# The softmax bias as a minimum of negatively scaled scores, with the query's norm held in that scale in the sparse attention

## The chip, the core and the metric

The kernel runs on one core of a Trainium2 chip. The core has a matrix engine (TensorE, "PE" in the rows; "PEld" is its weight load), a vector engine (VectorE, "DVE"), an activation engine (ScalarE, "ACT"), a slower general engine (GpSimd, "POOL") and queues that move data between main memory and the on-chip memory (SBUF); matrix products land in a small accumulator memory (PSUM). Each engine runs its own list of instructions in the order in which the program issued them, and waits where an operand or a buffer isn't ready. The metric is the device time of one execution in microseconds (us).

## What is computed

Two decoder layers on 256 tokens of width 1024, with 16 heads of 64. Layer 0 is a feed-forward half step, a mixture of three causal dilated attentions, and a feed-forward half step. A shared set of keys and values follows, and layer 1 is a feed-forward half step, native sparse attention (NSA: compressed, selected and sliding-window branches, two groups of key heads) and a last feed-forward half step. The lines that the change touches are these:

```python
# dilated attention: one softmax for each block of 128 queries
s = jnp.einsum('nhqd,nhkd->nhqk', qb, kb).astype(jnp.float32) * scale      # scale = 64 ** -0.5
s = jnp.where(band & (start - front + ki >= 0), s, -jnp.inf)
m = jnp.max(s, axis=-1, keepdims=True)
p = jnp.exp(s - m)
den = jnp.sum(p, axis=-1, keepdims=True)

# sparse attention: queries are normed per head, and a rotated copy feeds two of three branches
q = rms_norm(qg[..., :hdim].reshape(b, s, N_HEADS, HEAD_DIM), q_gain)
q_nope = to_grp(q)                 # compressed branch
q_rope = to_grp(rope(q))           # selected and sliding-window branches
ss = jnp.einsum('bkgqd,bkqnd->bkgqn', qr, ks).astype(jnp.float32) * scale
p_s = masked_softmax(ss, (kpos <= t[:, None])[:, :, None])
sw = jnp.einsum('bkgqd,bknd->bkgqn', qr, kw).astype(jnp.float32) * scale
p_w = masked_softmax(sw, wband & (start - SLIDE_WINDOW + ki >= 0))
```

The norm of a head is one number for each query and head: q times that number, then rotated, is the same as q rotated, then multiplied by it.

## The kernel before

Tokens lie on the 128 partitions in two tiles (`tt` or `qt`, 0 and 1). A matrix product of two float32 operands is made of three products of high and low parts, so each weight tile of 128x1024 needs a cast to its high part (ACT, line 387) and a subtraction for its low part (mostly DVE, line 413). These, and the reductions that form the adaptive scales from `w_ada` (DVE, line 393), are the background work between which all other DVE and ACT work stands.

**Order.** The program is written by a planner, class `_Clock`. A task is a generator that yields (engine, estimated time, buffers taken and given); the planner always steps the task that can start first by its estimates, and `pick` chooses among engines by the earliest estimated end. The order in which instructions are issued is each engine's final order. So an edit that alters one estimate or leaves out one step can move others.

**Dilated attention** (about 240 to 560 us of the span): for eight pairs of heads and two query tiles `dil_unit` makes two score tiles of 128x512 in PSUM; DVE adds the mask and takes the row maximum in one custom instruction each (line 975, with a second instruction that reads the accumulator out); DVE multiplies the two maxima by -SCALE into `nb` (line 980); ACT takes exp(SCALE·y + nb) (line 983); then 1/sum (989), scaling (991), transposes on PE (906) copied back by ACT (912) or DVE (914), and the value product (1007). `qk_task` prepares queries and keys of a head group: squares (ACT 860), sums (DVE 864), a root by three Newton steps of four POOL instructions (581, 584, 585, 586), the rotated copies (DVE 890, 894, POOL 895) scaled by that root on POOL (938), transposes on PE (906).

**Sparse attention** (about 980 to 1090 us): `q_task` handles a group of eight heads. It takes the squares and sums, runs the same Newton steps on POOL to `rs`, scales the queries for the compressed branch on DVE (N, inside line 1329) and transposes them (1348). For each token tile a `q_rope` task rotates the unnormed queries on DVE (890, 894, 895), waits until `rs` is there, scales the rotated copy (R, also line 1329, on POOL or DVE as `pick` finds), casts the high part on ACT (1379), subtracts for the low part (1383, POOL or DVE by `pick`) and transposes both (1389); PSUM is copied out by line 1358 on ACT or line 1360 on DVE, again by `pick`. `cmp_scores` does the compressed branch (PE 1406, DVE 1410 to 1427), which also needs the product of line 1531 (DVE). `units(kv)` starts eight `nsa_unit` tasks for each key group when both rotated tiles are ready: four score tiles (PE 1448, n = 128 or 256 columns), the mask and row maximum (DVE 1455), `nb` for all four (DVE 1458), exp (ACT 1461), 1/sum times a gate (DVE 1465, 1468), scaling by that (POOL 1478 or DVE 1475), transposes (PE 1485), value products (PE 1504).

Of the kernel before, what the change touches and what calls it, by code (L numbers as in the profile page):

```python
# [14 lines left out]
AF = mybir.ActivationFunctionType  # L15
ALU = mybir.AluOpType
# [34 lines left out]
RL = 0  # L51
# [12 lines left out]
P = 128  # L64
# [159 lines left out]
class _Kernel:  # L224
# [732 lines left out]
    def dil_unit(self, hg, hp, qt, oh, ol):  # L957
# [4 lines left out]
        mx, den = self.small(2, "mx"), self.small(2, "den")  # L962
# [340 lines left out]
    def q_task(self, kv, ps):  # L1303
# [15 lines left out]
        st = {"rs": None, "at": 0.0, "reads": 0}  # L1319
# [8 lines left out]
        def scaled(eng, o, i, tt):  # L1328
            eng.tensor_tensor(out=o, in0=i, op=ALU.mult,
                              in1=st["rs"][:, tt * 8:(tt + 1) * 8].unsqueeze(2).to_broadcast([P, 8, HD]))  # L1330

        for tt in range(TT):
            clk.spawn(self.q_rope(kv, tt, ps[tt], qr, st, read, scaled), RL)
        yield "G", 3200.0
        st["rs"] = self.head_newton(x, y, 16)
        st["at"] = clk.free["G"] + clk.lag
        N = []
        for tt in range(TT):
            yield "V", 610.0
            N.append(self.tmp((P, 8, HD)))  # L1340
            scaled(nc.vector, N[tt], ps[tt].rearrange("p (h d) -> p h d", d=HD), tt)
# [20 lines left out]
    def q_rope(self, kv, tt, ps, qr, st, read, scaled):  # L1362
# [73 lines left out]
    def nsa_unit(self, kv, pr, qt, oh, ol):  # L1436
# [15 lines left out]
        mx, den = self.small(4, "mx4"), self.small(4, "den4")  # L1452
# [407 lines left out]
```

## Time and profile before

| | |
|---|---|
| time before, median of 3 runs | 1301.76 us (1300.01 to 1302.33) |
| the profiled execution's own time | 1301.44 us |
| its span in the trace | 1299.7 us |
| PE, DVE, ACT, POOL busy | 1219.7 (94%), 975.8 (75%), 646.0 (50%), 258.0 us (20%) |
| span by stage | feed-forward 0 to 240, dilated 240 to 560, feed-forward, shared keys and feed-forward 560 to 980, sparse 980 to 1080, rest to 1299.7 |

The span is the stretch from the first to the last recorded instruction; 1.74 us of the execution's own time lie around it. All times below count from the span's start. In rows of instructions the columns are the start, the duration, engine, line and operation, the tiles written and read, shapes, and in brackets the engine's idle time before it with what released it.

### The profile page before, as it was taken

To read this page: it belongs to the slowest core of one execution; us is meant where nothing else is said; L and a number is where in the kernel's file an instruction comes from. 1 tells how busy PE (TensorE), PEld (TensorE's weight loads), DVE (VectorE), ACT (ScalarE), POOL (GpSimd) and SP (SyncE) were. 2 spreads that over 40 slices of the span, in tenths; PEclk is the share of its full clock that TensorE was granted. 3 is DMA by queue.
4 is the path that set the end of the run, shared out by engine and by line. 5 is a ranking of instruction groups with operands and counts; after the bars stand their busy time and mean duration, and the time that the engine had idled before them with its cause. 6 is when DMAs were issued, how large, how long until landed. Compare 5 with 4: busy or idle time off the path is not lost.

```text
span 1299.7 us, 23375 instructions
## 1 busy us (share of the span) xinstructions
PE 1219.7 (94%) x9373; PEld 1140.8 (88%) x9373; DVE 975.8 (75%) x1743; ACT 646.0 (50%) x1126; POOL 258.0 (20%) x356
## 2 busy tenths in 40 slices
PE   4799999789989898899999999999999889999998
PEld 3799999667777687799999999989998778999998
DVE  6799886866758677578888878878878997766652
ACT  4545454435445354456455446545435477654431
POOL 3480010462433525210000100030001353000000
PEclk9999999999899899899999999999999899999999
DMA  8889886543454534245988956776883003466650
GB/s 323 285 328 353 314 317 259 201 163 154 143 191 151 196 130 162 97 163 181 340 321 324 341 213 244 279 279 248 343 305 135 33 2 132 163 257 232 242 192 17
DMA packets 42733, 284.50 MB, mean 219 GB/s; under 512 B 5249, under 2 KB 6273, under 8 KB 9346
## 3 DMA queue, kind: packets, MB, share of 16 engines
q1 hardware_dynamic: 42626, 283.02, 58.9%
q8 instruction: 73, 1.20, 0.4%
q14 instruction: 34, 0.28, 0.1%
HBM read 281.96 MB, written 1.05 MB: 218 GB/s over the span
## 4 chain that ended last, share of the span: by engine, by line
PE 73%; DVE 12%; POOL 9%; ACT 3%; issue 2%; DMA 1%; SPq 0%; ACTq 0%; DVEq 0%; POOLq 0%
PE mm L466 18%; PE mm L467 18%; PE mm L468 18%; PE mm L849 3%; PE mm L850 3%; PE mm L851 3%; DVE wl L413 2%; POOL y L938 2%; PE tp L906 2%; POOL rs_t L584 2%; POOL rs_t L581 2%; POOL rs_y L586 2%; POOL rs_t L585 1%; DVE y L1455 1%; DVE st L393 1%
## 5 line engine op out<-in xcount | busy, mean ns | idle before, releaser
L413 DVE TENSOR_TENSOR wl<-st,wh 128x1024 fp32r<-128x1024 f32 x361 | 436.1, 1234 | 93.4 <-ACT wh L387 93.0
L387 ACT CAST wh<-st 128x1024 fp32r<-128x1024 f32 x361 | 369.0, 1049 | 133.8 <-PE mm L468 46.6
L466 PE MATMUL mm<-uh,wh 128*128 128x256 f32 x1304 | 364.6, 280 | 1.4 <-DVE y L738 1.4
L467 PE MATMUL mm<-uh,wl 128*128 128x256 f32 x1304 | 364.5, 280 | 0.0
L468 PE MATMUL mm<-ul,wh 128*128 128x256 f32 x1304 | 363.4, 279 | 0.0
L466 PEld LDWEIGHTS mm<-uh,wh 128*128 128x128 f32 x1304 | 245.0, 188 | 1.7 <-DVE y L738 1.6
L467 PEld LDWEIGHTS mm<-uh,wl 128*128 128x128 f32 x1304 | 245.1, 188 | 0.1
L468 PEld LDWEIGHTS mm<-ul,wh 128*128 128x128 f32 x1304 | 245.2, 188 | 0.0
L466 PE MATMUL mm<-y,wh 128*128 128x256 f32 x832 | 233.5, 281 | 0.1
L467 PE MATMUL mm<-y,wl 128*128 128x256 f32 x832 | 232.4, 279 | 0.0
L468 PE MATMUL mm<-y,wh 128*128 128x256 f32 x832 | 231.8, 279 | 0.0
L393 DVE CUSTOM_DVE_ANT_0 st<-st,cact 128x1024 f32<-128x1024 f32 x152 | 187.0, 1259 | 0.0
L466 PEld LDWEIGHTS mm<-y,wh 128*128 128x128 f32 x832 | 156.4, 188 | 1.1 <-issue 0.9
L467 PEld LDWEIGHTS mm<-y,wl 128*128 128x128 f32 x832 | 156.4, 188 | 0.0
L468 PEld LDWEIGHTS mm<-y,wh 128*128 128x128 f32 x832 | 156.4, 188 | 0.0
L849 PE MATMUL mm<-wh,uh 128*128 128x512 f32 (+1 forms) x336 | 137.1, 408 | 0.0
L850 PE MATMUL mm<-wl,uh 128*128 128x512 f32 (+1 forms) x336 | 132.4, 394 | 0.0
L851 PE MATMUL mm<-wh,ul 128*128 128x512 f32 (+1 forms) x336 | 131.7, 392 | 0.0
L524 POOL TENSOR_TENSOR y<-y 128x256 f32<-128x256 f32 x20 | 22.7, 1137 | 351.9 <-ACT y L505 351.9
L895 POOL TENSOR_TENSOR y<-y 128x512 f32<-128x512 f32 (+1 forms) x26 | 32.3, 1251 | 267.3 <-DVE y L894 157.2
L849 PEld LDWEIGHTS mm<-wh,uh 128*128 128x128 f32 x336 | 67.2, 200 | 14.2 <-issue 1.3
L851 PEld LDWEIGHTS mm<-wh,ul 128*128 128x128 f32 x336 | 66.9, 199 | 13.8
(254 smaller groups left out, 1622.0 us busy)
## 6 DMA issues: line engine op xcount, KB each, us to landing
st<-w_in SPq DMA_DIRECT2D x88, 1024.0 KB, 5.1
st<-w_ada SPq DMA_DIRECT2D x76, 1024.0 KB, 5.5
st<-w_out SPq DMA_DIRECT2D x44, 1024.0 KB, 6.4
st<-w_qk SPq DMA_DIRECT2D x24, 1024.0 KB, 4.9
st<-w_va SPq DMA_DIRECT2D x8, 1024.0 KB, 4.8
st<-w_o SPq DMA_DIRECT2D x8, 1024.0 KB, 4.9
st<-w_vb SPq DMA_DIRECT2D x4, 1024.0 KB, 5.5
st<-w_q SPq DMA_DIRECT2D x4, 1024.0 KB, 6.4
```

The costliest lines, as they stand in the source:

```text
L387: nc.scalar.copy(out=wh, in_=src)
L393: nc.vector.tensor_tensor_reduce(out=src, in0=src, in1=self.cact, scale=1.0, scalar=0.0, op0=ALU.mult, op1=ALU.add, accum_out=self.mod[:, ...
L413: (self.nc.gpsimd if eng == "G" else self.nc.vector).tensor_tensor(out=o, in0=src[:, c], in1=i.bitcast(F32), op=ALU.subtract)
L466: mm(out=out, lhsT=ah, rhs=bh, start=start, stop=False, **kw)
L467: mm(out=out, lhsT=al, rhs=bh, start=False, stop=False, **kw)
L468: mm(out=out, lhsT=ah, rhs=bl, start=False, stop=stop, **kw)
L581: eng.tensor_tensor(out=t, in0=y, in1=y, op=ALU.mult)
L584: eng.tensor_tensor(out=t, in0=t, in1=x, op=ALU.mult)
L849: mm(out=ps[tt], lhsT=uh[k][:, c], rhs=wh[:, o], start=k == 0, stop=False)
L850: mm(out=ps[tt], lhsT=uh[k][:, c], rhs=wl[:, o], start=False, stop=False)
L851: mm(out=ps[tt], lhsT=ul[k][:, c], rhs=wh[:, o], start=False, stop=k == KC - 1)
L895: (eng or nc.gpsimd).tensor_tensor(out=A, in0=A, in1=B, op=ALU.add)
```

## The change

In the dilated attention the masked score is now formed with the immediate scale -SCALE and reduced by a minimum, which is `nb` itself; the multiplication of line 980 is gone and the exponent's scale is -1. In the sparse attention the same happens with the scale read from a column of a table, `qscale`, which holds -SCALE times the query's root. The rotated queries aren't scaled any more: the rope task doesn't wait for the root, and units wait until `qscale` is written. POOL writes `qscale` in one 128x16 instruction behind the Newton steps. The queries of the compressed branch are scaled on DVE as before.

```diff
@@ dil_unit
-            nc.vector.tensor_tensor_reduce(out=st, in0=scs[e], in1=self.dmask[:, qt], scale=1.0, scalar=-3e38,
-                                           op0=ALU.add, op1=ALU.max, accum_out=mx[:, e:e + 1])
+            nc.vector.tensor_tensor_reduce(out=st, in0=scs[e], in1=self.dmask[:, qt], scale=-SCALE, scalar=3e38,
+                                           op0=ALU.add, op1=ALU.min, accum_out=nb[:, e:e + 1])
             sts.append(st)
             T = clk.V(512, clk.now)
-        nb = self.small(2, "nb")
-        nc.vector.tensor_scalar(out=nb, in0=mx, scalar1=-SCALE, scalar2=None, op0=ALU.mult)
-        T = clk.on("V", 70, T)
         for e in range(2):
-            nc.scalar.activation(out=sts[e], in_=sts[e], func=AF.Exp, bias=nb[:, e:e + 1], scale=SCALE,
+            nc.scalar.activation(out=sts[e], in_=sts[e], func=AF.Exp, bias=nb[:, e:e + 1], scale=-1.0,
@@ q_task
         yield "G", 3200.0
-        st["rs"] = self.head_newton(x, y, 16)
-        st["at"] = clk.free["G"] + clk.lag
+        rs = self.head_newton(x, y, 16)
+        nc.gpsimd.tensor_scalar(out=self.qscale[kv], in0=rs, scalar1=-SCALE, scalar2=None, op0=ALU.mult)
+        self.scaled[kv] = True
@@ q_rope
-        while st["rs"] is None or clk.now < st["at"]:
-            yield st["at"] if st["rs"] else clk.now + 100.0
-        w = clk.pick(0, G=1010.0, V=610.0)
-        yield w
-        scaled(nc.vector if w[0] == "V" else nc.gpsimd, R, R, tt)
@@ nsa_unit
+        head = qt * 8 + pr * 2
         for e, b, c, i in blocks:
-            nc.vector.tensor_tensor_reduce(out=sts[e][:, c], in0=scs[e][:, c], in1=self.amask[:, S - n:S], scale=1.0,
-                                           scalar=-3e38, op0=ALU.add, op1=ALU.max, accum_out=mx[:, i:i + 1])
-        nb = self.small(4, "nb4")
-        nc.vector.tensor_scalar(out=nb, in0=mx, scalar1=-SCALE, scalar2=None, op0=ALU.mult)
+            nc.vector.tensor_tensor_reduce(out=sts[e][:, c], in0=scs[e][:, c], in1=self.amask[:, S - n:S],
+                                           scale=self.qscale[kv][:, head + e:head + e + 1],
+                                           scalar=3e38, op0=ALU.add, op1=ALU.min, accum_out=nb[:, i:i + 1])
@@ units
-            while self.ready[kv] < TT or not self.keys:
+            while self.ready[kv] < TT or not self.scaled[kv] or not self.keys:
```

Where instructions stand now, by engine. Line numbers shift: 1217 before is 1214 after, 1348 is 1343, 1389 is 1379, 1383 is 1373, 1406 is 1396, 1448 is 1438, 1478 is 1468, 1485 is 1475, 989 is 986, 991 is 988. Over the whole program DVE issues 1701 instructions instead of 1743, among them 32 fewer `nb` and three fewer PSUM copies of line 1360 (ACT takes these); one unit's four multiplications (1475) and one pair of subtractions (1383) go from DVE to POOL.

**PE in the sparse attention, behind the second projection of queries.** Before, eight transposes of one unit and four of the next, of 128 columns (1485, one row of twelve), stand ahead of the compressed scores (1406):

```order
L1217 MATMUL tp<-ident,y 128x128 x2
L849 MATMUL mm<-wh,uh 128x512
L850 MATMUL mm<-wl,uh 128x512
L851 MATMUL mm<-wh,ul 128x512
L1448 MATMUL sc<-shareA,y 128x512
L1448 MATMUL sc<-y 128x512
L1448 MATMUL mm<-shareA,y 128x512
L1448 MATMUL mm<-y 128x512
L1485 MATMUL tp<-ident,y 128x128 x12
L1406 MATMUL sc<-shareB,y 128x32 x8
L1348 MATMUL tp<-ident,y 128x128 x4
L1389 MATMUL tp<-ident,y 128x128 x4
```

and after:

```order
L1214 MATMUL tp<-ident,y 128x128 x2
L1438 MATMUL sc<-shareA,y 128x512
L1438 MATMUL sc<-y 128x512
L1438 MATMUL mm<-shareA,y 128x512
L1438 MATMUL mm<-y 128x512
L1475 MATMUL tp<-ident,y 128x128 x8
L1379 MATMUL tp<-ident,y 128x128 x4
L1396 MATMUL sc<-shareB,y 128x32 x8
L1343 MATMUL tp<-ident,y 128x128 x4
L1379 MATMUL tp<-ident,y 128x128 x4
L1438 MATMUL sc<-shareA,y 128x256
```

The first four transposes of the rotated queries (1389, after 1379) have moved ahead of the compressed scores and ahead of the normed queries' transposes (1348); the next unit's four transposes have left this place.

**POOL at the same place**, the end of the Newton steps (rs_t, rs_y) and what stands behind. Before:

```order
L586 TENSOR_TENSOR rs_y_11372<-rs_t_11370,rs_y_11366 128x16
L581 TENSOR_TENSOR rs_t_11376<-rs_y_11372 128x16
L584 TENSOR_TENSOR rs_t_11376<-rs_t_11376,qkx 128x16
L585 TENSOR_SCALAR rs_t_11376<-rs_t_11376 128x16
L586 TENSOR_TENSOR rs_y_11378<-rs_t_11376,rs_y_11372 128x16
L1329 TENSOR_TENSOR y<-y,rs_y_11378 128x512 x2
L1478 TENSOR_TENSOR y<-y,rd_11516 128x512 x2
```

and after:

```order
L581 TENSOR_TENSOR rs_t_11321<-rs_y_11317 128x16
L584 TENSOR_TENSOR rs_t_11321<-rs_t_11321,qkx 128x16
L585 TENSOR_SCALAR rs_t_11321<-rs_t_11321 128x16
L586 TENSOR_TENSOR rs_y_11323<-rs_t_11321,rs_y_11317 128x16
L1329 TENSOR_SCALAR qscale_10695<-rs_y_11323 128x16
L1373 TENSOR_TENSOR y<-y 128x4x64 x2
L1468 TENSOR_TENSOR y<-y,rd_11361 128x256 x2
L1468 TENSOR_TENSOR y<-y,rd_11452 128x512 x2
```

The scaling of the rotated queries is gone; `qscale` and one pair of subtractions (1383, now 1373), which DVE did, stand behind the Newton steps. The products of the next unit (1478, now 1468, 128x256), which stood right ahead of the first Newton instruction, are behind those now. On DVE the sums that start the Newton steps (864, 877, 879) have moved ahead of the two products of line 1531, which stood ahead of them.

**DVE in the dilated attention, at about 403 us.** Before, from `nb` on:

```order
L980 TENSOR_SCALAR nb<-mx 128x2
L914 COPY y<-tp 128x512
L413 TENSOR_TENSOR wl<-st,wh 128x1024
L276 TENSOR_TENSOR y<-o,y 128x256
L989 RECIPROCAL rd<-den 128x2
L991 TENSOR_SCALAR y<-y,rd 128x512 x2
L413 TENSOR_TENSOR wl<-st,wh 128x1024
L393 ISA st,mod<-st,cact 128x1024
```

and after, from the same place:

```order
L914 COPY y<-tp 128x512
L413 TENSOR_TENSOR wl<-st,wh 128x1024 x2
L276 TENSOR_TENSOR y<-o,y 128x256
L986 RECIPROCAL rd<-den 128x2
L988 TENSOR_SCALAR y<-y,rd 128x512 x2
L393 ISA st,mod<-st,cact 128x1024
L393 ISA mod 128x1
```

The second weight subtraction (413) has moved from behind the scaling of line 991 to ahead of line 276. Elsewhere in the dilated attention the order on DVE differs at two more places, by one weight subtraction each, and is otherwise the same without `nb`.

## Rows read from the trace of the kernel before

**Rows 1.** Windows: us, PE, PEld, DVE, ACT, POOL busy, PEclk, DMA share, GB/s.

```profile
240.00:560.00 320.00, 283.64 (x1582) 229.71 (x1583) 217.79 (x394) 140.08 (x253) 135.08 (x192) 0.94 0.44 161
1020.00:1080.00 60.00, 49.60 (x426) 41.31 (x424) 54.09 (x221) 41.49 (x152) 29.71 (x42) 0.89 0.01 1
1080.00:1300.00 220.00, 215.52 (x1842) 214.25 (x1840) 136.03 (x193) 105.27 (x151) 5.66 (x5) 1.00 0.51 182
```

**Rows 2.** Waits of PE, whole span: us in total, times, longest.

```profile
PE tp L906 <- POOL y L938: 34.3, 15, 7.6
```

**Rows 3.** Chain of work that ended last, dilated stage: start, us, what.

```profile
550.17 0.18 DVE nb L980
```

**Rows 4.** Timeline of DVE and ACT, dilated stage, 396 to 410 us.

```profile
396.57 1.99 ACT L387 CAST wh<-st 128x1024 fp32r<-128x1024 f32 x2
404.23 1.62 DVE L413 TENSOR_TENSOR wl<-st,wh 128x1024 fp32r<-128x1024 f32 x1
407.21 0.42 DVE L276 TENSOR_TENSOR y<-o,y 128x256 fp32r<-128x256 f32 x1 [1.36 <-ACT y L275]
408.54 1.22 DVE L413 TENSOR_TENSOR wl<-st,wh 128x1024 fp32r<-128x1024 f32 x1
```

**Rows 5.** Timeline of PE, dilated stage, 418 to 432 us.

```profile
428.20 0.66 PE L906 MATMUL tp<-ident,y 128*128 128x128 f32 x4 [1.56 <-POOL y L938]
430.18 1.11 PE L906 MATMUL tp<-ident,y 128*128 128x128 f32 x4 [1.32 <-POOL y L938]
```

**Rows 6.** DVE groups by form, whole span: busy us, mean ns, idle before.

```profile
L980 DVE TENSOR_SCALAR nb<-mx 128x2 f32<-128x2 f32 x16 | 2.7, 169 | 0.6
L1458 DVE TENSOR_SCALAR nb<-mx 128x4 f32<-128x4 f32 x16 | 5.8, 360 | 0.6
L1360 DVE COPY y<-tp 128x512 f32<-128x512 f32 x10 | 6.6, 681 | 0.0
L1475 DVE TENSOR_SCALAR y<-y,rd 128x128 f32<-128x128 f32 x4 | 0.9, 277 | 0.0
L1383 DVE TENSOR_TENSOR y<-y 128x256 f32<-128x256 f32 x8 | 3.1, 437 | 0.0
```

**Rows 7.** DVE groups by form again: the reduction, and two nearest forms.

```profile
L1455 DVE CUSTOM_DVE_ANT_0 y<-sc,shareB 128x256 f32<-128x256 f32 x16 | 6.1, 417 | 0.0
L635 DVE SCALAR_TENSOR_TENSOR y<-y,sh 128x256 fp32r<-128x256 f32 x8 | 3.8, 480 | 0.4 <-ACT y L643 0.2
L738 DVE TENSOR_TENSOR y<-y,mm 128x256 f32<-128x256 f32 x84 | 35.0, 417 | 32.1 <-ACT y L737 32.0
```

**Rows 8.** Timeline, sparse stage: one long bias and POOL beside it.

```profile
1040.76 2.04 POOL L1478 TENSOR_TENSOR y<-y,rd 128x512 f32<-128x512 f32 x2 [8.06 <-DVE rd L1468]
1041.99 0.82 DVE L1458 TENSOR_SCALAR nb<-mx 128x4 f32<-128x4 f32 x1
```

**Rows 9.** Timeline of PE, sparse stage, behind the query projection.

```profile
1025.44 0.97 PE L1485 MATMUL tp<-ident,y 128*128 128x128 f32 x4 [1.05 <-POOL y L1478]
1026.24 2.62 PE L1406 MATMUL sc<-shareB,y 128*128 128x32 f32 x16
1031.44 1.09 PE L1348 MATMUL tp<-ident,y 128*128 128x128 f32 x4 [2.58 <-DVE y L1329]
1034.05 0.58 PE L1448 MATMUL sc<-shareA,y 128*128 128x256 f32 x1
```

**Rows 10.** Timeline of POOL and DVE, sparse stage, around the Newton steps.

```profile
1026.27 0.21 POOL L581 TENSOR_TENSOR rs_t<-rs_y 128x16 f32<-128x16 f32 x1 [0.36 <-DVE rs_y L879]
1030.65 2.04 POOL L1329 TENSOR_TENSOR y<-y,rs_y 128x512 f32<-128x512 f32 x2
1022.23 2.07 DVE L1531 TENSOR_TENSOR y<-shareB,bdm 128x512 f32<-128x512 f32 x2
```

**Rows 11.** Timeline of POOL, the first Newton steps of the dilated stage.

```profile
247.04 1.12 POOL L581 TENSOR_TENSOR rs_t<-rs_y 128x16 f32<-128x16 f32 x1 [0.32 <-DVE rs_y L879]
255.14 1.07 POOL L586 TENSOR_TENSOR rs_y<-rs_t,rs_y 128x16 f32<-128x16 f32 x1
```

More of the change, by code (lines that the diff above doesn't have):

```diff
@@ L961, in dil_unit @@
         mm = nc.tensor.matmul
-        mx, den = self.small(2, "mx"), self.small(2, "den")
+        nb, den = self.small(2, "nb"), self.small(2, "den")
         scs, sts = [], []
@@ L1318, in q_task @@
         y = self.head_seed(x, 16)
-        st = {"rs": None, "at": 0.0, "reads": 0}
+        st = {"rs": None, "reads": 0}
         def read():
@@ L1326, in read @@
                     clk.pool["sc"] += [clk.now + 500.0] * 2
-        def scaled(eng, o, i, tt):
-            eng.tensor_tensor(out=o, in0=i, op=ALU.mult,
-                              in1=st["rs"][:, tt * 8:(tt + 1) * 8].unsqueeze(2).to_broadcast([P, 8, HD]))
         for tt in range(TT):
-            clk.spawn(self.q_rope(kv, tt, ps[tt], qr, st, read, scaled), RL)
+            clk.spawn(self.q_rope(kv, tt, ps[tt], qr, read), RL)
         yield "G", 3200.0
-        st["rs"] = self.head_newton(x, y, 16)
-        st["at"] = clk.free["G"] + clk.lag
+        rs = self.head_newton(x, y, 16)
+        nc.gpsimd.tensor_scalar(out=self.qscale[kv], in0=rs, scalar1=-SCALE, scalar2=None, op0=ALU.mult)
+        self.scaled[kv] = True
         N = []
@@ L1340, in q_task @@
             N.append(self.tmp((P, 8, HD)))
-            scaled(nc.vector, N[tt], ps[tt].rearrange("p (h d) -> p h d", d=HD), tt)
+            nc.vector.tensor_tensor(out=N[tt], in0=ps[tt].rearrange("p (h d) -> p h d", d=HD), op=ALU.mult,
+                                    in1=rs[:, tt * 8:(tt + 1) * 8].unsqueeze(2).to_broadcast([P, 8, HD]))
             read()
@@ L1360, in copy, with q_rope @@
             self.nc.vector.tensor_copy(out=o, in_=i)
-    def q_rope(self, kv, tt, ps, qr, st, read, scaled):
+    def q_rope(self, kv, tt, ps, qr, read):
         nc, clk = self.nc, self.clk
@@ L1451, in nsa_unit @@
         yield "V", 4 * (1.04 * n + 70) + 200, {}, {"sc": 2}
-        mx, den = self.small(4, "mx4"), self.small(4, "den4")
+        nb, den = self.small(4, "nb4"), self.small(4, "den4")
         sts = [self.tmp() for _ in range(2)]
+        head = qt * 8 + pr * 2
         for e, b, c, i in blocks:
-            nc.vector.tensor_tensor_reduce(out=sts[e][:, c], in0=scs[e][:, c], in1=self.amask[:, S - n:S], scale=1.0,
-                                           scalar=-3e38, op0=ALU.add, op1=ALU.max, accum_out=mx[:, i:i + 1])
-        nb = self.small(4, "nb4")
-        nc.vector.tensor_scalar(out=nb, in0=mx, scalar1=-SCALE, scalar2=None, op0=ALU.mult)
+            nc.vector.tensor_tensor_reduce(out=sts[e][:, c], in0=scs[e][:, c], in1=self.amask[:, S - n:S],
+                                           scale=self.qscale[kv][:, head + e:head + e + 1],
+                                           scalar=3e38, op0=ALU.add, op1=ALU.min, accum_out=nb[:, i:i + 1])
         yield "A", 4 * (0.84 * n + 280)
@@ L1461, in nsa_unit @@
             nc.scalar.activation(out=sts[e][:, c], in_=sts[e][:, c], func=AF.Exp, bias=nb[:, i:i + 1],
-                                 scale=SCALE, accum_out=den[:, i:i + 1])
+                                 scale=-1.0, accum_out=den[:, i:i + 1])
         yield "V", 350.0
@@ L1523, in nsa_mixer @@
         self.taken, self.blocks = [False, False], False
+        self.scaled = [False, False]
+        self.qscale = [self.const(f"qscale{i}", [P, 16]) for i in range(2)]
         def compressed(kv):
```

## The prediction

> **What bounds the kernel now.** I read the busy time by stage first [rows 1]. Behind 1080 us PE works 215.5 of 220 us, and the change touches nothing there, so only the two attentions can give or take. In the dilated stage PE works 283.6 of 320 us: 36.4 us idle. The list of PE's waits says for what: 34.3 us of its waits, in 15 places, are transposes of a head group's queries and keys that wait for POOL's scaling [rows 2]. That scaling stands behind the Newton steps, these behind DVE's sums, and the sums behind a queue of weight subtractions and reductions on DVE. A step on DVE that lies ahead of the sums moves PE; one behind them doesn't. In the sparse stage, 1020 to 1080 us, DVE is busy 54.1 of 60 us and PE 49.6, so PE has 10.4 us to lose [rows 1]: DVE is the bound, with PE's and POOL's hand-overs between. I work the sum against the profiled execution, 1301.44 us, of which 1.74 us lie around the span; it stands 0.32 us under the median of the runs, so an improvement of 3 us reads as 3.3 against the median.
>
> **The change, dilated attention.** Removed are 16 instructions of 0.17 us, 2.7 us together [rows 6]. ACT's exponent follows `nb`, so each chain from scores to exponent is shorter by its length and a gap of 0.02 to 0.03, some 0.20 us. The chain that ended last does run through it, for instance at 550.17 us with 0.18 [rows 3]. But 16 × 0.20 = 3.2 us would need every step to be on the path, and mostly DVE goes straight on to a weight subtraction while PE has other products; so the bounds are 0 and 3.2. I take 0.7, nearer to none: three or four of the 16, since two units run beside each other and the next wait of PE is that for POOL. The scale becomes another immediate in the same instruction and the reduction a minimum; both cost nothing.
>
> The order moves at one place that matters. Before, DVE does one subtraction at 404.23, then idles 1.36 us for ACT until 407.21, and does the next one behind that, at 408.54, for 1.22 us [rows 4]. After, both stand ahead of line 276. The second needs a cast that ACT finished before 399 (two casts from 396.57, 1.99 us [rows 4]), so it fits into the idle time. It leaves the queue ahead of the sums, which start the Newton steps for which PE then waits 1.56 and 1.32 us, 2.88 together [rows 5]. The step of one subtraction is about 1.14 us; I take 1.1. The bounds are 0 (the subtraction is held up, as the 1.62 us at 404.23 was, and only swaps places) and 1.4 (the whole idle). At the two other places a weight subtraction swaps with a neighbour of its size: 0, ±0.5. **The dilated sum is −1.8 us**, from +0.5 to −5.1.
>
> **The change, sparse attention, DVE's work.** Less: 16 `nb`, 5.8 us busy [rows 6]. Of these the short ones take 0.17; the mean of 0.36 comes from a few that took as long as 0.82 us because POOL's products ran beside them [rows 8]. Such a wait may pass on to the next instruction, so only 16 × 0.17 = 2.7 us is sure, and 5.8 the upper end. Further, three PSUM copies go to ACT, 3 × 0.68 = 2.0; four multiplications of one unit to POOL, 4 × 0.28 = 1.1; one pair of subtractions to POOL, 2 × 0.44 = 0.9 (all [rows 6]). That is 6.7 us sure and 9.8 at most.
>
> More: each of 64 reductions now reads its scale from a column instead of an immediate. No reduction of the trace does. The nearest rows are three-operand instructions with a column scalar, 480 ns on 128x256, and the two-operand form without one, 417, which is also what the reduction takes now [rows 7]. So 63 ns each, 64 × 63 = 4.0 us. The lower bound is 0 (the reduction's own 417), the upper 4.0, as no row makes a column dearer; below 0 nothing, since the elements and passes are the same. I take 4.0: it is the one pair of rows that differs in this. **DVE's net is then −2.7 (6.7 − 4.0)**, from −9.8 to −2.7.
>
> **Sparse attention, what is late next.** PE's list is the part that can cost. Before, PE did a unit's four transposes and the compressed scores (from 1025.44 to 1028.9) while POOL ran the Newton steps, then waited 2.58 us for the normed queries; the next unit's scores began at 1034.05 [rows 9]. After, the first thing behind the eight transposes (they end at 1024.4, where the wait of 1.05 ends at 1025.44 [rows 9]) are the rotated queries' four, and these need POOL's subtraction, which now stands behind twelve Newton instructions and `qscale`. When? The Newton steps began at 1026.27 and ended at 1030.6: 4.3 us for twelve. Their sums now go ahead of line 1531's two products, which took 2.07 [rows 10], so they may begin 2 us earlier, at 1024.3, and end at 1028.6; `qscale` is one more of 0.2, and the pair of subtractions about 1.0 (half of the 2.04 that POOL took for two of twice the size [rows 10]): 1029.8. If the two products of line 1531, now beside the Newton steps, hold two of its instructions at 1.1 us instead of 0.2 [rows 11], it is 1031.6. I take 1030.6.
>
> PE's idle time up to there is then 6.2 us instead of 1.05 + 2.58 = 3.6. Behind it PE still has the 2.6 us of compressed scores and the eight transposes [rows 9], some 2 us, ahead of the next unit's scores: 1030.6 + 1.0 + 2.6 + 2 = 1036.2 instead of 1034.05, 2.2 late. DVE has other work for most of that time; it reaches these scores only behind a queue of its own. So the cost lies between 0 and 2.2, and I take 1.4, nearer to the upper end because the compressed scores now come late too and the units' last step waits for them. The removed scaling of the rotated queries (2.04 us on POOL [rows 10]) helps here only in that the subtraction no longer waits for it; that is in the times above. The new wait of the units for `qscale` costs nothing: it is one instruction of 0.2 us behind steps for which they waited before. DVE is busy 54.1 of 60 us, so I count nine tenths of its 2.7 as on the path, 2.4. **The sparse sum: −2.4 + 1.4 = −1.0 us**, from +2.2 (nothing of DVE's on the path) to −9.8 (all of the upper end, none of PE's order).
>
> *A rule of the skill beside this.* The rows show Newton instructions of 1.05 to 1.12 us where others take 0.21, eight in a row from 247.04 to 255.14 [rows 10, 11]. The Trainium skill, SBUF — State Buffer, § Who interferes with whom, says that DVE and GpSimd share a port pair as an exclusive lock: an instruction of DVE with two SBUF inputs holds off GpSimd's reads, one with at most one doesn't outside the two-port modes. The trace agrees where DVE's weight subtractions run beside the Newton steps. By that rule the products of line 1531 (two SBUF inputs) do hold two of them, 1031.6 is right and the sum 1.0 us higher; it speaks against the change, which puts PE behind that very list. By the same rule a long `nb` takes its wait with it if what follows on DVE reads PSUM, which is the second rival.
>
> **The sum: 1301.44 − 1.8 − 1.0 = 1298.6 us.**
>
> **The rivals.**
> 1. *The column price and the order eat the gain.* PE's order costs its 2.2, DVE's 2.7 is only partly on the path, and in the dilated stage the moved subtraction just swaps places: 1301.44 − 2.4 + 2.2 − 0.5 = 1300.7. That is the case in which the change does not do what it says: the multiplication is gone but the 64 reductions carry its cost. For it: the two prices (4.0 against 2.7 sure). Against: the idle of 1.36 us is there to be filled.
> 2. *The waits go with `nb`.* The whole 9.8 − 4.0 = 5.8 us leaves DVE: 1301.44 − 1.8 − 5.8 + 1.4 = 1295.2. For it: the long ones stand beside POOL's products [rows 8]. Against: POOL's products are still there and now more of them.
> 3. *PE stands behind POOL.* If the Newton steps run as at 247 to 256 us, eight in a row with 0.88 us more each [rows 11], the rotated queries' transposes start 7 us later and everything behind them on PE too: 1298.6 + 7.0 = 1305.6. It decides against the change from four such instructions on (2.8/0.88 = 3.2). For it: DVE's list behind the sums begins with two-input products, and rotations follow. Against: before, the twelve at this place took 4.3 us together, and DVE's list beside them is as short of weight subtractions after as before.
>
> **How the numbers follow.** The likeliest is the forecast, .45, with its own range of 1296.8 to 1300.5: down by 1.8 if most of the dilated `nb` count (2.5 instead of 0.7), up by 1.9 if PE's order costs 2.2 instead of 1.4 and the moved subtraction gives nothing of its 1.1. The second rival has .16, the first .27, the third .12. About 0.2% of the median, 2.6 us, is what a measurement of this kernel can tell from no change, so faster means below 1299.2 and slower above 1304.4. Of the forecast's .45 some three quarters lie below 1299.2, with the second rival's .16 this is .50; the rest of the forecast and the first rival make .38; the third .12. The range of 1294.5 to 1303 takes in the forecast and two rivals and leaves out most of the third.
>
> **What would show it.** Right: no line between reduction and exponent; the waits for line 938 at about 428 us shorter by 1 us; reductions of 128x256 in the sparse stage at some 0.48 us (0.42 would say that the column is free); the first transposes of the rotated queries at about 1030.6; PE's idle in the sparse stage near 9 us. Wrong: these transposes later than 1033, a new long wait of PE on POOL's subtraction, or a dilated stage as long as before. What would make it wrong altogether: the planner's new order stalling at a place that I read as neutral.

## The result and the profile after

The changed kernel takes 1310.30 us (median of 6 runs, 1310.07 to 1311.57) against 1302.42 us of before on the same chip (1300.01 to 1304.52): a ratio of 1.0068, with a 95% interval of 1.0055 to 1.0080, so 7 to 10 us slower. The prediction was 1298.6 us, faster, with a range of 1294.5 to 1303.0. It was wrong in sign and in range.

The timeline of PE has three waits that stand at the same step of the program in both kernels: the first head group's transposes, the gates' transposes ahead of the sparse attention, and the last unit's transposes in it. Of before:

```profile
258.57 1.69 PE L906 MATMUL tp<-ident,y 128*128 128x128 f32 x6 [7.60 <-POOL y L938]
1006.47 0.32 PE L1294 MATMUL tp<-ident,y 48*128 48x48 f32 x2 [1.18 <-ACT y L1290]
1073.41 0.63 PE L1485 MATMUL tp<-ident,y 128*128 128x128 f32 x4 [2.09 <-DVE rd L1465]
```

and of after:

```profile
259.83 2.12 PE L906 MATMUL tp<-ident,y 128*128 128x128 f32 x8 [7.61 <-POOL y L938]
1014.39 0.32 PE L1291 MATMUL tp<-ident,y 48*128 48x48 f32 x2 [1.21 <-ACT y L1287]
1083.13 0.73 PE L1475 MATMUL tp<-ident,y 128*128 128x128 f32 x4 [2.09 <-ACT y L1353]
```

After is 1.3 us late at the first, where the change has not acted yet: some 100 us in, PE waited 1.0 us for a subtraction of DVE, a delay that two of the first four experiments below show and two don't, with the same program there. It is 7.9 us late at the second and 9.7 at the third; the spans differ by 10.1. So **the dilated stage lost some 6.6 us and the sparse stage 2 to 2.5.** Both were to gain.

The windows that answer [rows 1]: the dilated stage of after over a stretch of the same length, eight us later, and a stretch of the sparse stage of after from the gates' transposes on:

```profile
248.00:568.00 320.00, 282.37 (x1553) 228.13 (x1554) 212.43 (x369) 135.35 (x246) 133.76 (x190) 0.91 0.42 155
1014.40:1096.40 82.00, 68.64 (x557) 59.24 (x558) 66.41 (x249) 54.00 (x185) 32.09 (x47) 0.92 0.08 27
```

The same sparse stretch of before, with as many matmuls (558 and 557), which [rows 1] doesn't have whole:

```profile
1006.50:1086.00 79.50, 69.10 (x558) 58.22 (x560) 68.68 (x273) 51.22 (x181) 30.90 (x44) 0.91 0.05 15
```

From the first head group's transposes to the last value product of the dilated stage PE runs the same 1543 matmuls; of before, then of after:

```profile
258.57:560.60 302.03, 273.27 (x1543) 221.94 (x1543) 203.42 (x373) 132.96 (x244) 121.99 (x177) 0.94 0.42 155
259.83:568.50 308.67, 278.64 (x1543) 225.70 (x1543) 203.08 (x357) 133.45 (x244) 123.20 (x177) 0.91 0.41 151
```

And PE's waits of after, which answer [rows 2]:

```profile
PE tp L906 <- POOL y L938: 36.6, 14, 7.6
...
PE tp L1379 <- POOL y L1373: 6.4, 1, 6.4
```

Read these three things. DVE's busy time in the sparse stage fell by 2.3 us (68.7 to 66.4) and the stage got 2.5 longer all the same: DVE's work was not what set its length. The wait for POOL in the dilated stage grew, from 34.3 to 36.6 us. And the granted clock of that stage fell from 0.94 to 0.91 of full speed: of the 6.6 us that the same 1543 matmuls take longer, 5.4 are PE's busy time and only 1.3 its idle time. In this execution, then, most of the loss shows as work at the lower clock. In the execution of the kernel with the new order alone (the fourth experiment) it is the other way round: of 6.6 us, 4.9 are idle time and 1.6 busy time.

The place that the prediction costed, at 404 to 418 us before, with the reduction at its head and the sums at its end; on DVE, before:

```profile
402.05 0.69 DVE L975 CUSTOM_DVE_ANT_0 y<-sc,shareB 128x512 f32<-128x512 f32 x1 [1.16 <-PE sc L969]
...
418.80 1.26 DVE L864 TENSOR_REDUCE qkx<-y 128x8 f32<-128x512 f32 x2
```

and after:

```profile
404.05 0.69 DVE L975 CUSTOM_DVE_ANT_0 y<-sc,shareB 128x512 f32<-128x512 f32 x1 [1.32 <-PE sc L969]
...
406.22 3.45 DVE L413 TENSOR_TENSOR wl<-st,wh 128x1024 fp32r<-128x1024 f32 x2
409.60 0.41 DVE L276 TENSOR_TENSOR y<-o,y 128x256 fp32r<-128x256 f32 x1
...
417.83 0.69 DVE L890 TENSOR_TENSOR y<-mm,shareA 128x512 f32<-128x512 f32 x1 [0.45 <-ACT y L860]
...
420.36 1.26 DVE L864 TENSOR_REDUCE qkx<-y 128x8 f32<-128x512 f32 x2
```

The idle time ahead of line 276 [rows 4] is filled, as foreseen. But of what the queue gains there it loses 0.45 us at 417.83, where DVE now stands idle until ACT's squares of the new projection (860) are there, and these follow PE. Counted from line 975 the sums come 16.31 us later instead of 16.75: 0.44 us earlier, two missing bias steps (`nb`) included, where 1.1 was forecast for the subtraction alone. With the new order and the bias steps kept, the same distance is 17.29 us, 0.54 more than before. So the sums were not late because of this one subtraction.

The Newton steps and the transposes behind them, which answer [rows 5]; POOL, then DVE, then PE, after:

```profile
425.96 1.08 POOL L584 TENSOR_TENSOR rs_t<-rs_t,qkx 128x16 f32<-128x16 f32 x1
427.13 1.05 POOL L585 TENSOR_SCALAR rs_t<-rs_t 128x16 f32<-128x16 f32 x1
428.57 3.92 POOL L938 TENSOR_TENSOR y<-y,rs_y 128x512 f32<-128x512 f32 x2
```

```profile
425.12 0.69 DVE L914 COPY y<-tp 128x512 f32<-128x512 f32 x1 [0.80 <-PE tp L906]
425.72 1.24 DVE L413 TENSOR_TENSOR wl<-st,wh 128x1024 fp32r<-128x1024 f32 x1
426.88 1.24 DVE L393 CUSTOM_DVE_ANT_0 st<-st,cact 128x1024 f32<-128x1024 f32 x1
```

```profile
430.55 0.66 PE L906 MATMUL tp<-ident,y 128*128 128x128 f32 x4 [3.05 <-POOL y L938]
432.54 1.12 PE L906 MATMUL tp<-ident,y 128*128 128x128 f32 x4 [1.32 <-POOL y L938]
```

PE waits 3.05 us where it waited 1.56. Each Newton instruction of POOL takes 0.2 us, or 1.05 to 1.08 where DVE's two-input instructions run beside it: the two rows of POOL lie under DVE's 413 and 393 and end 0.06 to 0.08 us behind them. Before, DVE's copy came later against the Newton steps (with 1.52 us of idle ahead of it, as the timeline of before has it), and the pair of subtractions behind it met only the last of them:

```profile
424.26 0.69 DVE L914 COPY y<-tp 128x512 f32<-128x512 f32 x1 [1.52 <-PE tp L906]
424.87 2.37 DVE L413 TENSOR_TENSOR wl<-st,wh 128x1024 fp32r<-128x1024 f32 x2
...
424.98 1.18 POOL L586 TENSOR_TENSOR rs_y<-rs_t,rs_y 128x16 f32<-128x16 f32 x1
```

In the sparse stage, PE and POOL after, which answer [rows 9] and [rows 10]:

```profile
1038.69 1.11 PE L1379 MATMUL tp<-ident,y 128*128 128x128 f32 x4 [6.42 <-POOL y L1373]
1039.59 3.46 PE L1396 MATMUL sc<-shareB,y 128*128 128x32 f32 x16
...
1044.46 0.56 PE L1438 MATMUL sc<-shareA,y 128*128 128x256 f32 x1
```

```profile
1032.41 0.59 POOL L581 TENSOR_TENSOR rs_t<-rs_y 128x16 f32<-128x16 f32 x1 [0.99 <-DVE rs_y L879]
...
1037.69 0.26 POOL L1329 TENSOR_SCALAR qscale<-rs_y 128x16 f32<-128x16 f32 x1
1037.90 1.41 POOL L1373 TENSOR_TENSOR y<-y 128x256 f32<-128x256 f32 x2
```

The rotated queries' transposes wait 6.42 us for POOL's subtraction; the forecast had 6.2. The next unit's scores begin 30.1 us behind the gates' transposes where they began 27.6 us behind them: 2.5 late, where the prediction worked out 2.2 and took 1.4.

The reductions with a column, which answer [rows 7]:

```profile
L1446 DVE CUSTOM_DVE_ANT_0 y<-sc,shareB,qscale 128x256 f32<-128x256 f32 x16 | 7.0, 475 | 0.8 <-PE sc L1438 0.8
...
L1446 DVE CUSTOM_DVE_ANT_0 y<-sc,shareB,qscale 128x128 f32<-128x128 f32 x16 | 4.9, 345 | 1.3 <-PE sc L1438 1.3
```

475 ns instead of 417 and, on 128x128, 345 instead of the 284 that an immediate took: 58 and 61 ns each, 3.8 us over 64, where the forecast had 63 ns and 4.0 us.

### The profile page after: what moved, and what is told of

Read it like the earlier page. It is cut to its first block, busy times and chain, and to the rows that moved or that the text cites. A ratio compares the mean times of both kernels' runs of the same rounds, so it can differ in the third digit from the quotient of the medians.

```text
span 1309.8 us, 23365 instructions
## 1 busy us (share of the span) xinstructions
PE 1226.6 (94%) x9373; PEld 1147.4 (88%) x9373; DVE 969.6 (74%) x1701; ACT 646.8 (49%) x1129; POOL 256.7 (20%) x359
## 3 DMA queue, kind: packets, MB, share of 16 engines
HBM read 281.96 MB, written 1.05 MB: 216 GB/s over the span
## 4 chain that ended last, share of the span: by engine, by line
PE 73%; DVE 11%; POOL 9%; ACT 4%; issue 2%; DMA 1%; SPq 0%; ACTq 0%; DVEq 0%; POOLq 0%
PE mm L466 17%; PE mm L467 17%; PE mm L468 17%; PE mm L849 3%; PE mm L850 3%; PE mm L851 3%; DVE wl L413 3%; PE tp L906 2%; POOL rs_t L581 2%; POOL rs_y L586 2%; POOL rs_t L584 2%; DVE st L393 2%; POOL y L938 1%; POOL rs_t L585 1%; DVE qkx L864 1%
```

## Experiments

Every ratio is against the kernel before, run beside it on the same chip (medians of 1300.5 to 1300.8 us), with its 95% interval. Where two experiments are compared, the difference of their ratios is taken times 1300 us, also where they ran on different chips; such a difference is uncertain by some 2 to 4.5 us.

### The parts, and in the dilated part order against instructions

The dilated part alone (the changed `dil_unit` in the kernel before), and the sparse part alone (all other hunks).

> The dilated part of the change alone, the sparse attention as before. In the trace of the changed kernel PE's milestones fall back by 6.7 us between 240 and 560 us and by 2.6 between 980 and 1090. If the two parts act apart, this run is 5.5 to 7 us slower than before (ratio 1.0042 to 1.0054). If most of the dilated loss were chance of one execution, it would be within 2 us of before.

Measured: 1305.91 us, 1.0051 (1.0030 to 1.0072), 6.6 us slower.

> The sparse part alone, the dilated attention as before. If the parts act apart: 2 to 3 us slower than before. If the dilated part were chance of one execution, this one carries most of the 8 us.

Measured: 1304.11 us, 1.0026 (1.0014 to 1.0039), 3.4 us slower. The parts add up to the whole: 10.0 against 8.9, well inside the intervals.

The dilated part does two things: it drops 16 instructions, and it no longer counts 70 ns for each in the planner, which gives another order. The two can be had apart. First the instructions dropped and the count kept (every engine's order in the stage is then that of before without `nb`):

```diff
             T = clk.V(512, clk.now)
+        T = clk.on("V", 70, T)
         for e in range(2):
             nc.scalar.activation(out=sts[e], in_=sts[e], func=AF.Exp, bias=nb[:, e:e + 1], scale=-1.0,
```

> The dilated part, with the planner still counting 70 ns for the multiplication that is gone, so that every engine issues in the order of before and only the 16 multiplications are missing. Theory of the order (the moved weight subtractions cost the time): 0.5 to 2 us faster than before. Rival, the missing step itself (queues run 0.2 us earlier against POOL, which meets DVE elsewhere): 4 to 7 us slower.

Measured: 1298.20 us, 0.9980 (0.9966 to 0.9993), 2.6 us faster.

And the kernel before with the count dropped, the instructions kept:

```diff
         nc.vector.tensor_scalar(out=nb, in0=mx, scalar1=-SCALE, scalar2=None, op0=ALU.mult)
-        T = clk.on("V", 70, T)
```

> The kernel before with one edit: the planner doesn't count the 70 ns, so the order is that of the changed dilated part while the 16 multiplications and the old reductions stay. Theory of the order: 5.5 to 8 us slower than before. Rival, the missing step: within 2 us of before.

Measured: 1307.36 us, 1.0047 (1.0025 to 1.0069), 6.1 us slower. So the arithmetic of the change is a gain of 2.6 us in the dilated stage, and **the order that the planner makes of 70 ns is a loss of 6.1**; together they predict 3.5 and gave 6.6, which the intervals allow.

In the new order a part of DVE's weight subtractions stands elsewhere, and at seven places of PE's list a projection triple (three products, 0.7 us) has moved, at most of them behind transposes that it stood ahead of. The traces count what this does to POOL. This table is worked out from the rows of the Newton steps: the time from the first of a group's twelve instructions to the end of the last, and how many of the twelve took more than 0.45 us.

| head group's step | before | instructions dropped, old order | instructions kept, new order | the change |
|---|---|---|---|---|
| 4th (of 12) | 4.34 us, 1 held | 4.42, 1 | 3.49, 0 | 3.50, 0 |
| 8th | 5.46, 2 | 4.50, 1 | 7.98, 5 | 6.22, 3 |
| 10th | 3.48, 0 | 3.48, 0 | 4.46, 1 | 4.47, 1 |
| 11th | 7.83, 5 | 7.94, 5 | 8.69, 6 | 8.69, 6 |

The length is 3.5 us plus 0.85 to 1.0 for each held instruction, and executions with the same order and instructions in this stage agree to 0.03 us. The other eight groups keep their counts. Over the whole stage 48 of 144 Newton instructions are held before, 50 in the change and 52 with the instructions kept; every one of them ran beside a subtraction of line 413 or a reduction of line 393. So the new order adds four held instructions on balance with the old instructions and three without the bias steps, 3.5 and 2.5 us on POOL; in the fourth group it takes one away. In the eighth group of the kernel with the new order and the old instructions, DVE's copy has 0.27 us of idle ahead of it instead of 1.52, since PE's transposes come a triple earlier and the sums, counted from line 975, 0.54 us later; the weight subtractions then run under the Newton steps, five are held, and PE waits 5.33 us in one piece:

```profile
424.70 0.69 DVE L914 COPY y<-tp 128x512 f32<-128x512 f32 x1 [0.27 <-PE tp L906]
425.31 1.22 DVE L413 TENSOR_TENSOR wl<-st,wh 128x1024 fp32r<-128x1024 f32 x1
```

```profile
425.48 1.12 POOL L586 TENSOR_TENSOR rs_y<-rs_t,rs_y 128x16 f32<-128x16 f32 x1
426.68 1.07 POOL L581 TENSOR_TENSOR rs_t<-rs_y 128x16 f32<-128x16 f32 x1
...
428.14 1.08 POOL L585 TENSOR_SCALAR rs_t<-rs_t 128x16 f32<-128x16 f32 x1
429.30 1.07 POOL L586 TENSOR_TENSOR rs_y<-rs_t,rs_y 128x16 f32<-128x16 f32 x1
```

```profile
432.40 1.90 PE L906 MATMUL tp<-ident,y 128*128 128x128 f32 x7 [5.33 <-POOL y L938]
```

DVE's copy, done sooner, made the Newton steps later. The Trainium skill, SBUF — State Buffer, § Who interferes with whom, says that a DVE instruction with two SBUF inputs contends with a GpSimd instruction that reads SBUF. These rows agree: POOL's instructions take 1.07 to 1.12 us beside DVE's subtractions and reductions of 1.22 to 1.24 us, and 0.2 to 0.3 us elsewhere.

### What the new order costs by PE's triples and by held Newton steps

First the triples: at four head groups the task is resumed 200 ns later in the planner, which puts PE's triple back ahead of the waiting transposes at three of them and changes no other engine's order.

```diff
-        yield T
+        yield T + (200.0 if n in (7, 8, 9, 10) else 0.0)
```

> The kernel with the new order in the dilated stage and the old instructions (6.9 us slower than before), with one edit: at three head groups the planner resumes the queries' and keys' task 200 ns later, so that one projection triple on PE (three products, 0.7 us) stands again ahead of the transposes that wait for POOL, as before; DVE's and POOL's order stay the new one. If the cost sits in PE's order (a wait that is 0.7 us less filled, three times): 2 to 4 us faster than without the edit, so 3 to 5 us slower than before. If it sits in the Newton steps on POOL, which DVE's moved instructions hold up (five held instead of two in one group, six instead of five in another): within 1 us of the kernel without the edit, so 6 to 8 us slower than before.

Measured: 1304.70 us, 1.0030 (1.0016 to 1.0043), 3.9 us slower than before, so these three triples are some 2.2 of the 6.1. Four of the seven moves on PE and all of DVE's stay as in the new order. The counts of held steps stay at 5, 1 and 6. PE's long wait is shorter by 0.9:

```profile
430.59 0.81 PE L906 MATMUL tp<-ident,y 128*128 128x128 f32 x4 [4.44 <-POOL y L939]
```

Then Newton steps that can't be held: on DVE, for the three groups of the table.

```diff
-        rs = self.head_rstd(x, 16)
+        rs = self.head_rstd(x, 16, nc.vector if n in (7, 9, 10) else None)
```

> The kernel before with the Newton steps of three head groups only (the 8th, 10th and 11th of the twelve) on DVE: those that the new order holds up more than the old one. The reference for the next run. By the trace the three take 5.5, 3.5 and 7.8 us on POOL, of which PE waits behind the first and the third: 6 to 12 us faster than before.

Measured: 1296.31 us, 0.9960 (0.9946 to 0.9974), 5.2 us faster than before.

> The new dilated order with the triples put back (0.3% or some 4 us slower than before) and the same three groups' Newton steps on DVE, where DVE can't hold them up. If the 4 us that are left of the new order are held Newton steps (5 instead of 2, 1 instead of 0, 6 instead of 5: 4.4 us by 0.87 each): 0 to 1.5 us slower than the run with the old order and the three groups on DVE. If they are something else, DVE's own queue say: 3 to 5 us slower than it.

Measured: 1297.72 us, 0.9980 (0.9967 to 0.9993). It is 2.6 us by ratios, 1.4 by medians, behind its reference, where 3.9 were left with the steps on POOL. So held steps are about 1.3 us of the rest by ratios, 2.5 by medians, and 1 to 3 us sit elsewhere; the intervals overlap, so that neither share is shown to differ from none.

All twelve groups' steps on DVE, in the old and in the new order (orders of all engines otherwise unchanged):

```diff
-        rs = self.head_rstd(x, 16)
+        rs = self.head_rstd(x, 16, nc.vector)
```

> The kernel before with the Newton steps of the dilated stage on DVE instead of POOL (nine instructions of some 0.17 us behind the sums, where POOL took 3.5 to 10.4 us), every engine's order otherwise unchanged. If POOL's held Newton steps set PE's waits there (34 us in 15 places), these shrink by more than half, and the kernel gets 15 to 30 us faster. If DVE's own queue or POOL's scaling behind the steps sets them: within 5 us of before.

Measured: 1261.61 us, 0.9705 (0.9683 to 0.9727), 38 us faster, more than the 15 to 30 of the theory. PE's waits of the dilated stage in that kernel:

```profile
PE tp L906 <- DVE y L991: 4.4, 6, 1.4
PE mm L849 <- DVE y L894: 2.8, 2, 1.7
PE mm L850 <- DVE wl L413: 2.2, 2, 1.9
PE tp L906 <- POOL y L938: 1.9, 4, 0.8
```

The wait for POOL fell from 34.3 us to 1.9. DVE took nine instructions of 0.17 to 0.18 us where POOL took twelve of 0.2 or 1.1, and the whole step, 1.8 us, stands right behind the sums. So these steps on POOL, held or not, made nearly all of PE's waits there.

> The same move of the Newton steps in the kernel with the new order in the dilated stage. If that order costs its 6.9 us by holding up Newton steps on POOL, nothing can be held any more: within 1.5 us of the kernel before with its Newton steps on DVE. If it costs by PE's triples alone: 2 to 4 us slower than that one.

Measured: 1267.63 us, 0.9738 (0.9720 to 0.9756): 4.3 us slower than in the old order. No step is held on POOL here, so the expectation for held steps alone (within 1.5) is missed, though the interval of the difference reaches down to it; the one for the triples alone (2 to 4) is nearer. By the runs, then, the 6.1 us of the new order are about 2 of triples, 1 to 2 of held steps and 1 to 3 that these experiments don't place: the other moves on PE, those on DVE, and the time at the lower clock are left for it. Each share is as uncertain as it is large, and the intervals of the two last runs overlap a little.

### The clock

In the dilated stage the granted clock stands at 1.2 instead of 2.4 GHz in stretches behind PE's waits: it is 0.50 of full speed from 430 to 432 us of before and from 432 to 438 us of after, behind the waits of 1.56 and 3.05 us. Work that computes nothing was put ahead of nine of the waiting transposes, sized to end before POOL does:

```diff
         tp = self.pst()
+        for i in range(warm):
+            nc.tensor.transpose(out=tp[:, 0:P], in_=self.ident, identity=self.ident)
```

> The kernel before, with work added that computes nothing: ahead of the transposes of a head group's queries and keys that wait for POOL's scaling, PE transposes the identity 8 to 50 times into the same PSUM tile, 182 in all, sized to end before the scaling does. If PE's work behind these waits is slow because the clock stands at 1.2 GHz there (34 us at that level in the dilated stage of the kernel before), the granted clock stays at 1.00 and the kernel gets 5 to 12 us faster. If the clock costs little, or PE isn't the bound behind the waits: within 2 us of before, or slower where the added work is too long.

Measured: 1291.77 us, 0.9926 (0.9902 to 0.9950), 9.6 us faster with 182 matmuls more. (At a mean granted clock of 0.94 the 320 us of [rows 1] hold (1 − 0.94) × 2 × 320 = 38 us at the lower level, not the 34 of the expectation.) Thirty us from the eighth group's wait on in the two kernels (us, PE, PEld, DVE, ACT, POOL busy, PEclk); before:

```profile
427.00:457.00 30.00, 23.89 (x115) 19.95 (x115) 19.35 (x28) 11.92 (x23) 15.54 (x18) 0.89 0.60 213
```

and with the added work:

```profile
426.00:456.00 30.00, 26.51 (x157) 22.34 (x158) 20.35 (x28) 12.76 (x24) 15.88 (x18) 1.00 0.62 226
```

> The same added work in the kernel whose only edit is the new order in the dilated stage (6.9 us slower than before without it). If the new order costs by its longer waits alone, some 3 to 5 us, it stays 3 to 5 us slower than the kernel before with the same added work. If it costs mainly by stretches at 1.2 GHz, 0 to 2 us slower.

Measured: 1301.67 us, 1.0008 (0.9994 to 1.0022): 10.7 us behind the old order with the same added work, worse than either expectation. The same thirty us:

```profile
424.00:454.00 30.00, 23.00 (x108) 18.67 (x107) 15.09 (x25) 8.75 (x18) 17.81 (x22) 0.89 0.54 208
```

The added work was sized for the old waits. In the new order what is left of the wait is 4.3 us at this place, the clock falls as before, and PE pays there for the wait and for the work behind it at half speed. Over the whole stage the two traced executions differ by 6.6 us (306.9 against 313.5, from 247.5 us on), of which PE's idle time is 5.2 and its busy time for the same 1742 matmuls 1.4. So in these two the longer waits are most of it; why the medians stand 10.7 us apart is not shown.

> The dilated part of the change in the order of before, 2.3 us faster than before by itself, with the same added work. If the two act apart: 2 to 3 us faster than the kernel before with added work.

Measured: 1290.82 us, 0.9916 (0.9890 to 0.9941), 1.3 us ahead of the kernel before with added work by ratios; the intervals overlap, so this settles nothing on whether the two add.

### The sparse part

The sparse part's PE order was put back at one place: the rotated queries' transposes of the second key group wait in the planner until the first group's compressed scores are issued.

```diff
+        while kv and not self.scored:
+            yield clk.now + 100.0
         for i in range(2):
             yield "P", 440.0, {"tp": 1}
```

> The sparse part alone (3.4 us slower than before), with one more edit: the rotated queries' transposes of the second key group wait in the planner until the compressed scores of the first are issued, so that these 2.6 us stand again ahead of them on PE, where they fill PE's wait for POOL. Theory of the order on PE: 1.5 to 3 us faster than the sparse part alone, so 0.5 to 2 us slower than before. Rival, the price of the column and POOL's products behind the Newton steps: it stays 3 to 4 us slower than before.

Measured: 1300.40 us, 0.9999 (0.9986 to 1.0013): 3.5 us faster than the sparse part alone, as fast as before. PE in that kernel:

```profile
1025.68 1.87 PE L1401 MATMUL sc<-shareB,y 128*128 128x32 f32 x16
1032.04 1.09 PE L1346 MATMUL tp<-ident,y 128*128 128x128 f32 x4 [4.49 <-DVE rd L1461]
```

The compressed scores run inside the wait again, which is 4.49 us for what was 6.42, and the next unit's scores begin 26.8 us behind the gates' transposes instead of 30.1: 3.3 us earlier. The planner then orders later instructions otherwise too (PE's list differs from that of the sparse part alone at a dozen places, nearly all behind this one), so the run prices the place with what follows from it. Within the interval that is all of the sparse part's loss.

The price of the column, with the query's norm left out of two branches:

```diff
-                                           scale=self.qscale[kv][:, head + e:head + e + 1],
+                                           scale=-SCALE,
```

> The sparse part alone with the compressed scores first (as before in time, 0.9999), with an immediate scale -SCALE in the 64 reductions instead of a column; the query's norm is left out of two branches, so this only prices the column. In the trace a column reduction takes 475 ns against 417 (128x256) and 344 against 284 (128x128), 3.8 us in all. If DVE bounds the stage: 2 to 4 us faster than with the column. If other waits bound it: within 1 us.

Measured: 1302.04 us, 0.9999 (0.9985 to 1.0014). In the trace the reduction is back at 416 and 284 ns, and the time doesn't move: the two runs, whose orders are the same, differ by 0 us with an interval of 2.6 us to either side, so the 3.8 us of DVE's work were not all on the path, and by the best estimate none of them.

### The repaired change, and with the Newton steps on DVE

Both orders put back, the whole arithmetic of the change kept:

> The whole change with both orders put back: the planner still counts 70 ns in the dilated unit, and the compressed scores stand ahead of the rotated queries' transposes. If the two parts act apart, and what slowed the change is order alone: 2 to 3 us faster than before (the dilated part in the old order gave 2.3, the sparse part with its scores first 0.1). If the arithmetic itself costs (the column, POOL's table): as before or slower.

Measured: 1298.81 us, 0.9981 (0.9969 to 0.9993), 2.5 us faster than before and 11 faster than the change as it was made.

> The repaired change with all Newton steps of the dilated stage on DVE, which alone made the kernel before 39 us faster. If the gains add: 40 to 43 us faster than before. If the bias step that the change saves lay on the path only through POOL's waits: as the kernel before with its Newton steps on DVE, 38 to 40 us faster.

Measured: 1258.64 us, 0.9672 (0.9654 to 0.9689), 43 us faster than before. The gain of the repaired change seems to stand beside that of the Newton steps (0.9705 without it), though the intervals still overlap. This is the fastest of all.

## Why the prediction was wrong

**Which engine bounds.** The stage view was right for the dilated stage: PE waits for POOL behind a chain over DVE. For the sparse stage it was wrong. DVE's 54.1 of 60 us [rows 1] were read as the bound; 2.3 us less of DVE's work gave nothing, and an immediate in place of the column neither. PE's wait for POOL at one place was the stage's price.

**Dilated, the missing bias step: −0.7.** The mechanism was right and the size too small. In the old order it gave −2.6 (−0.9 to −4.4), near the 3.2 that the prediction had for "every step to be on the path"; by its interval it may also be as little as 0.9. The forecast counted a step only where the chain passes through it; the trace shows one more way: with one instruction fewer, the eighth group's Newton steps had one held instead of two (4.50 us instead of 5.46).

**Dilated, the moved subtraction: −1.1.** This failed. The subtraction does fill the idle time, but the sums come only 0.44 us earlier in the change and 0.54 later with the bias steps kept, since DVE then idles for ACT's squares, which follow PE's projection. The chain of waits of before went through DVE's subtractions there, and the prediction took each of them as the cause; nothing was said of what would be late next, though in the trace of before ACT's squares end at 416.16 us, 0.1 us ahead of the rotation on DVE (890, at 416.26) that leads to the sums.

**Dilated, "at the two other places ... 0, ±0.5". This is the step that made the sign wrong.** It compared sizes of neighbours on DVE and no more. DVE's order differs at three other places (323, 426 and 487 us of before), not at two. Two things were missed: at seven places of PE's list a triple moved against its neighbours, and what DVE runs in the few us of the Newton steps decides how long POOL takes for them. Measured for the order as a whole: +6.1 us (3 to 9), of which the runs place about 2 with three triples and 1 to 2 with held steps; the rest stays open. The triples' moves stood in the order of before and after as plainly as DVE's, and weren't weighed.

**Sparse, PE's order: +1.4, between 0 and 2.2.** Place, cause and times were right: transposes at 1030.6, in the run of the sparse part at 1030.2; scores 2.2 late, measured 2.5. Its size was cut to 1.4 because "DVE has other work". That work was not the bound, so the whole of it counted: putting the order back gave 3.5 us.

**Sparse, DVE's net: −2.4.** Each price was good: 58 to 61 ns for the column against 63. What failed is the factor of nine tenths for the path. DVE's busy time did fall, by 2.3 us where 2.7 were worked out, and with PE's place put back the time was still that of before (0.9999, 0.9986 to 1.0013): the whole −2.4 is missing.

**The rivals.** The third rival named a mechanism that the dilated stage shows, Newton steps of 1.05 to 1.12 us instead of 0.2, and put it in the sparse stage, where only four of twelve are longer than 0.45 us, at 0.55 to 0.73 us, and the steps take 5.2 us. Of its "four such instructions" of 0.88 us more none came there. They came in the dilated stage, three to four more on balance, behind places that were called neutral, and by the runs they are 1 to 2 us of the 6.1. Its chance of .12 was too small mainly because it was asked of one stage only. The prediction also took the clock as a given: it has no term for PE's work at the lower level, and in the traced execution of the change that is 5.4 of the 6.6 us that the dilated stage lost. How much of it the new order brings, and how much differs between executions of one order, is not shown.

## What to carry to other kernels

Where a planner writes the order, an edit's own cost can be a few us and the order that follows from it more, with the other sign; take them apart by keeping the old estimate in the planner, which costs one line. Before costing a gain on a queue, look for what releases the next instruction once the queue is empty. And where a slow engine's short instructions lie on the path, ask whether they could stand on the fast engine at all: that was worth 38 us here, and the change under study, with both orders put back, 2.5.

## What the runs showed of the hardware

- A POOL instruction on 128x16 of 0.2 us takes 1.05 to 1.2 us while DVE runs subtractions and reductions with two 128x1024 inputs, and a chain of twelve goes from 3.5 to as much as 10.4 us (before, eight held); the same Newton steps as nine instructions on DVE take 1.8.
- Idle time of PE can cost more than itself: with 182 transposes that compute nothing in PE's waits the granted clock of the 30 us behind one of them was 1.00 instead of 0.89, and the kernel got 9.6 us faster.
- A scale read from a column costs this reduction 58 to 61 ns on 128 and on 256 elements alike, so here it is a price per instruction.
- Executions of one kernel differ by several us in the dilated stage, since the stretches at 1.2 GHz don't last equally long in each: the repaired change took 312.9 us from its first Newton step to its last value product, the same instructions in the same order beside the old sparse part 307.7 (granted clock 0.92 and 0.94 over these stretches, PE busy 279.7 and 273.0 us). A profile of one execution can't settle 5 us there.
